# A decoder layer on one core: convolution states turned by full 128-row tiles, a padded sample residual, and engine orders fixed by tables

## The chip, the cores and the metric

The kernel runs on one core of a Trainium2 chip. The metric is device time in microseconds (us) of one launch. Three runs of the kernel before took 900.96, 899.11 and 896.12 us, so 899.11 us in the median. The profiled execution is a fourth one.

TensorE is called PE here, VectorE DVE, ScalarE ACT, GpSimd POOL and SyncE SP; PEld is PE's loading of the operand that stays in the array.

## What is computed

One layer of a hybrid decoder for a prompt of 512 tokens and 8 sample tokens (one new token for each of 8 sequences), width 1024, all in fp32. Cut to its frame:

```python
# x: prompt (1, 512, 1024) and sample (8, 1, 1024); the two groups share all weights
u = x @ w_in                                 # queries, keys, values, gates of both mixers
nsa = sparse_attention(u)                    # compressed, selected and window branches, ALiBi
qkv, gdn_conv = causal_dwconv(u_qkv, state_gdn_conv, width=4)     # state: 3 rows of 1536 per sequence
gdn, gdn_state = gated_delta_net(silu(qkv), state_gdn)            # 8 heads of 64, chunks of 64
x = layer_norm(ALPHA * x + concat(nsa, gdn) @ w_out)
h, ffn_conv = causal_dwconv(x @ w_up, state_ffn_conv, width=3)    # state: 2 rows of 2816 per sequence
x = layer_norm(ALPHA * x + (gelu(h) * gate) @ w_down)
x = layer_norm(ALPHA * x + per_layer_embedding(x, p))
# outputs: x, key/value rows, windows, delta-net states, the new rows of both convolutions
```

## The kernel before

**Layout.** Activations lie with features on the partitions and the 520 tokens along the columns, in two halves: half 0 has 256 columns (prompt), half 1 has 264 (256 of the prompt and the 8 samples). The weights come from HBM by feature tiles of 128.

**Products.** An fp32 product is made of three products in the faster type float32r. `wtile` casts a weight tile to `wh` (ACT, L210 or L199) and subtracts to get the rest `wl` (DVE or POOL, L211 or L200). `product` then does for each 128 rows of the contraction wh·xh (L355), wl·xh (L356) and wh·xl (L359). The steps that carry a page row name `mm` are these. Small products are left in fp32, which the trace shows as two records each.

**Order.** The work is written as a list of steps in two strings: `ORDER` (input projection tiles G and D, attention steps, delta-net steps K, g, C, X, s, v, then w_out) and `TAIL` (w_down tiles D, norms M, the embedding P and B, the last norm and the outputs). A table `do` calls a function for each step. That written order is not the order on the engines: `kernel` opens the tile framework with its scheduler, which reorders the written instructions of each engine by its own estimates and inserts the waits. Each engine then runs its own fixed list.

**Places that the change touches.**
- L266-267: the first piece of the delta-net's convolution state, 24 rows of 512, is loaded. `conv_state` (L401-409) loads the other two, turns each by four transposes of 24 rows x 128 columns (L408) into one PSUM tile `gstT`, and copies that to `gst`. `gdn_tile` calls it at its tiles 0, 4 and 8.
- `residual` (L1271-1281) adds ALPHA·x to an output tile inside PSUM, between two of the w_out steps: two fp32 products with 128 token rows against ALPHA times the identity `aid` (L1278, four records), and in half 1 one with the 8 sample rows (L1280, two records). There are 8 output tiles in each half. `delta_half` (L1283-1292) loads the sample rows as two tiles `xs` of 8 rows.
- `ffn_state` (L1346-1356) loads the ConvFFN's state as six pieces of 16 rows, turns it by 22 transposes of 16 rows x 128 columns (L1354) and copies each piece from PSUM (DVE, L1355, six copies).
- Three further places are only moved: the delta-net's key products `kk` on 32 rows (L589, L591), the norms (`mu` L1229, subtraction L1233, squares `lsq` L1235, `var` L1241, `rstd` L164, scaling L1250, the casts `x1h` L1252 and `x1l` L1254), and the delta-net's chunk steps on 64 rows (`vn` L763, `S` L769, `o` L784 and L792, `val` L719, `kcd` L728, `qk` L743, and the transposes of the keys and values L874).

Of the kernel before, what the change touches and what calls it, by code (L numbers as in the profile page):

```python
# [23 lines left out]
HA = 256  # L24
HEADS = 8
FF = 2816
NFT = FF // 128
# [70 lines left out]
SUB, EVAC = 'VVVVVVVV VVVVVVVV VVVVVVVV VVVVVVVV VVVVVVVV'.split(), 'VVVVVVVV VVVVVVVV'.split()  # L98
TAIL = 'D00 D10 D11 D12 D01 D13 D14 D15 D16 D17 M1 D02 P0 D03 D04 D05 B0 D06 B1 D07 B2 P1 M0 B3 B4 L B5 R0 B6 B7 T00 T01 Z E3 U0 R1 T10 T11 T12 U1 E2 E4'


def body(tc, nc, ctx, I, O, dbg=None):
# [22 lines left out]
    def PS(name, tag):  # L125
        nid[0] += 1
        return pp.tile([128, 512], F32, tag=tag, name=f"{name}_{nid[0]}", bufs=BANKS[tag])
# [19 lines left out]
    def r3(ap, n):  # L147
        return ap.rearrange("p (a b) -> p a b", a=n)
# [116 lines left out]
    rows_v = feature_rows()  # L265
    st_first = UV("st24", [24, 512])  # L266
    nc.sync.dma_start(st_first, I["state_gdn_conv"][0].rearrange("b r c -> (b r) c")[:, 512:1024])
    w_first = [([], [])]
# [128 lines left out]

    gst = UV("gst", [128, 12, 24])
    gstv = gst.rearrange("p j (b r) -> p j b r", r=3)

    def conv_state(hf):  # L401
        st = st_first
        if hf != 1:
            st = UV("st24", [24, 512])
            nc.sync.dma_start(st, I["state_gdn_conv"][0].rearrange("b r c -> (b r) c")[:, hf * 512:(hf + 1) * 512])
        ps = PS("gstT", "pn")
        for j in range(4):
            PE.transpose(ps[:, j * 24:(j + 1) * 24], st[:, j * 128:(j + 1) * 128], ident[:24, :24])  # L408
        V.tensor_copy(gst[:, hf * 4:(hf + 1) * 4, :], r3(ps[:, :96], 4))

# [50 lines left out]
    def gdn_tile(j, ws=None):  # L461
# [4 lines left out]
        if not F:  # L466
            vectors()
        if j % 4 == 0:
            conv_state(j // 4)
        gcw = F["gcw"]  # L470
# [803 lines left out]
    def residual(o, hv, rows):  # L1274

        def add(_, ps):
            for s2 in range(2):
                PE.matmul(ps[:, s2 * 128:s2 * 128 + 128], rows[:, s2 * 128:s2 * 128 + 128], L["aid"], start=False, stop=False)  # L1278
            if hv == 1:
                PE.matmul(ps[:, HA:HA + 8], xsrow[o], L["aid"][:8, :8], start=False, stop=False)  # L1280
        return add

    def delta_half(hv, tag):  # L1283
        if "aid" not in L:
            L["aid"] = UV("aid", [128, 128])
            G.tensor_scalar(L["aid"], ident, ALPHA, None, op0=ALU.mult)
        if hv == 1:
            rs_ = [UV("xs", [8, 512], "g") for c in range(2)]
            for c in range(2):
                nc.sync.dma_start(rs_[c], I["x_sample"][:, 0, c * 512:(c + 1) * 512])  # L1290
            xsrow[:] = [rs_[k // 4][:, k % 4 * 128:k % 4 * 128 + 128] for k in range(8)]
        split_mix(hv, tag, 1)
        R[hv] = by_halves("R", hv, "g")
# [52 lines left out]
    def ffn_state():  # L1346
        fst = UV("fst", [128, NFT, 16])
        for c0 in range(0, NFT, 4):
            n = min(4, NFT - c0)
            st = UV("st16", [16, 512])  # L1350
            nc.sync.dma_start(st[:, :n * 128], I["state_ffn_conv"][0].rearrange("b r c -> (b r) c")[:, c0 * 128:(c0 + n) * 128])
            ps = PS("fstT", "pg")
            for j in range(n):
                PE.transpose(ps[:, j * 16:(j + 1) * 16], st[:, j * 128:(j + 1) * 128], ident[:16, :16])  # L1354
            V.tensor_copy(fst[:, c0:c0 + n, :], r3(ps[:, :n * 16], n))  # L1355
        FS["v"] = fst.rearrange("p j (b r) -> p j b r", r=2)

# [290 lines left out]
```

## Time and profile before

| what | value |
|---|---|
| three runs | 900.96, 899.11, 896.12 us (median 899.11) |
| the profiled execution's own time | 898.38 us |
| its span (first to last instruction) | 896.4 us |
| its mean granted TensorE clock | 0.982 of full speed |
| PE busy | 862.4 us, 96% of the span |
| PEld busy | 804.2 us, 90% |
| DVE busy | 576.5 us, 64% |
| ACT busy | 426.8 us, 48% |
| POOL busy | 194.3 us, 22% |
| busy share of the 16 DMA engines, first queue | 32.6% |

How to read it: the time of a run is the span and about 2 us around it. Busy times are unions of instruction spans; a PE instruction's span is longer than the distance to the next one, since products are pipelined, so prices on PE are read as distances between starts. PEclk is the clock that was granted; 1.00 is full speed and 0.50 half.

### The profile page before, as it was taken

To read this page: it belongs to the slowest core of one execution; us is meant where nothing else is said; L and a number is where in the kernel's file an instruction comes from. 1 tells how busy PE (TensorE), PEld (TensorE's weight loads), DVE (VectorE), ACT (ScalarE), POOL (GpSimd) and SP (SyncE) were. 2 spreads that over 40 slices of the span, in tenths; PEclk is the share of its full clock that TensorE was granted. 3 is DMA by queue.
4 is the path that set the end of the run, shared out by engine and by line. 5 is a ranking of instruction groups with operands and counts; after the bars stand their busy time and mean duration, and the time that the engine had idled before them with its cause. 6 is when DMAs were issued, how large, how long until landed. Compare 5 with 4: busy or idle time off the path is not lost.

```text
span 896.4 us, 19333 instructions
## 1 busy us (share of the span) xinstructions
PE 862.4 (96%) x7689; PEld 804.2 (90%) x7689; DVE 576.5 (64%) x1317; ACT 426.8 (48%) x940; POOL 194.3 (22%) x301
## 2 busy tenths in 40 slices
PE   8999999999998989999999999999999999998995
PEld 6989998988897757979999999999999999998984
DVE  3788994576769787778655553345543345577967
ACT  4555546333447885645644432244431244434744
POOL 1241231362404432206720000000000000005333
PEclk9999999899999999989999999999999999999998
DMA  7322323332237230333413333333343134352202
GB/s 222 86 54 72 92 78 81 91 85 61 67 85 242 73 100 13 108 113 92 142 60 119 106 97 94 97 113 102 93 119 95 55 89 119 92 157 82 95 1 96
DMA packets 138550, 85.93 MB, mean 96 GB/s; under 512 B 8354, under 2 KB 129940, under 8 KB 138316
## 3 DMA queue, kind: packets, MB, share of 16 engines
q1 hardware_dynamic: 138460, 84.70, 32.6%
q8 instruction: 60, 0.98, 0.5%
q14 instruction: 30, 0.25, 0.1%
HBM read 79.48 MB, written 7.36 MB: 97 GB/s over the span
## 4 chain that ended last, share of the span: by engine, by line
PE 75%; DVE 9%; DMA 7%; ACT 5%; issue 2%; POOL 2%; SPq 1%; DVEq 0%; POOLq 0%; ACTq 0%
PE mm L355 19%; PE mm L359 18%; PE mm L356 18%; DMA wn<-in_state_nsa_win_dram 2%; PE PT L992 2%; DVE wl L211 1%; DMA praw<-in_ple_w_gate_dram 1%; DMA raw<-in_ffn_w_down_dram 1%; PE var L1241 1%; DMA raw<-in_w_out_dram 1%; PE O L999 1%; DVE R L1250 1%; PE O L1000 1%; DMA raw<-in_ffn_w_up_dram 1%; PE S L956 1%
## 5 line engine op out<-in xcount | busy, mean ns | idle before, releaser
L211 DVE TENSOR_TENSOR wl<-raw,wh 128x512 fp32r<-128x512 f32 (+1 forms) x190 | 132.5, 700 | 131.0 <-ACT wh L210 129.9
L210 ACT CAST wh<-raw 128x512 fp32r<-128x512 f32 x198 | 120.3, 612 | 189.6 <-PE mm L359 152.3
L356 PE MATMUL mm<-x1h,wl 128*128 128x256 f32 (+1 forms) x704 | 199.0, 283 | 0.4 <-POOL wl L211 0.4
L359 PE MATMUL mm<-x1l,wh 128*128 128x256 f32 (+1 forms) x704 | 198.7, 283 | 0.0
L355 PE MATMUL mm<-x1h,wh 128*128 128x256 f32 (+1 forms) x704 | 198.4, 283 | 0.0
L356 PEld LDWEIGHTS mm<-x1h,wl 128*128 128x128 f32 x704 | 132.1, 188 | 0.9 <-POOL wl L211 0.8
L359 PEld LDWEIGHTS mm<-x1l,wh 128*128 128x128 f32 x704 | 132.6, 188 | 0.1
L355 PEld LDWEIGHTS mm<-x1h,wh 128*128 128x128 f32 x704 | 132.5, 189 | 0.1
L355 PE MATMUL mm<-xh,wh 128*128 128x264 f32 (+1 forms) x408 | 120.4, 295 | 1.7 <-ACT xh L329 1.0
L359 PE MATMUL mm<-xl,wh 128*128 128x264 f32 (+1 forms) x408 | 118.8, 291 | 0.0
L356 PE MATMUL mm<-xh,wl 128*128 128x264 f32 (+1 forms) x408 | 118.3, 290 | 0.0
L356 PE MATMUL mm<-hhl,wl 128*128 128x256 f32 (+1 forms) x352 | 100.0, 286 | 0.0
L355 PE MATMUL mm<-hhl,wh 128*128 128x264 f32 (+1 forms) x352 | 100.0, 286 | 0.0
L359 PE MATMUL mm<-hhl,wh 128*128 128x256 f32 (+1 forms) x352 | 99.7, 286 | 0.0
L355 PEld LDWEIGHTS mm<-xh,wh 128*128 128x128 f32 x408 | 78.9, 193 | 3.7 <-ACT xh L329 1.1
L359 PEld LDWEIGHTS mm<-xl,wh 128*128 128x128 f32 x408 | 78.8, 193 | 0.9 <-issue 0.5
L356 PEld LDWEIGHTS mm<-xh,wl 128*128 128x128 f32 x408 | 78.8, 193 | 0.8 <-issue 0.5
L1392 POOL COPY last<-fcb 128x10 f32<-128x10 f32 x22 | 4.9, 225 | 307.9 <-ACT fcb L1380 296.5
L355 PEld LDWEIGHTS mm<-hhl,wh 128*128 128x128 f32 x352 | 66.9, 191 | 0.2
L356 PEld LDWEIGHTS mm<-hhl,wl 128*128 128x128 f32 x352 | 66.9, 190 | 0.2
L359 PEld LDWEIGHTS mm<-hhl,wh 128*128 128x128 f32 x352 | 66.5, 190 | 0.2
L1255 POOL TENSOR_SCALAR R<-R,vec 128x264 f32<-128x264 f32 (+1 forms) x40 | 32.2, 817 | 49.9 <-ACT x1h L1252 34.6
(450 smaller groups left out, 1879.4 us busy)
## 6 DMA issues: line engine op xcount, KB each, us to landing
raw<-in_ffn_w_up_dram SPq DMA_DIRECT2D x44, 512.0 KB
raw<-in_w_in_dram SPq DMA_DIRECT2D x25, 512.0 KB
raw<-in_w_out_dram SPq DMA_DIRECT2D x32, 256.0 KB
raw<-in_ffn_w_down_dram SPq DMA_DIRECT2D x16, 512.0 KB
pg<-in_cache_nsa_kv_dram SPq DMA_DIRECT2D x16, 256.0 KB
praw<-in_ple_w_gate_dram SPq DMA_DIRECT2D x8, 512.0 KB
raw<-in_ffn_w_down_dram SPq DMA_DIRECT2D x8, 384.0 KB
xr<-in_x_prompt_dram SPq DMA_DIRECT2D x16, 128.0 KB
```

What stands on the lines that cost most here:

```text
L210: both = (S.copy(th[:, :k1 - k0, :M], raw[:, k0:k1, :M]), low.tensor_tensor(tl[:, :k1 - k0, :M], raw[:, k0:k1, :M], th[:, :k1 - k0, :M], o ...
L211: low.tensor_tensor(tl[:, :k1 - k0, :M], raw[:, k0:k1, :M], th[:, :k1 - k0, :M], op=ALU.subtract))
L355: PE.matmul(o, hs[k], rh[hv][k], start=(k == ks[0]), stop=False)
L356: PE.matmul(o, ls[k], rh[hv][k], start=False, stop=False)
L359: PE.matmul(o, hs[k], rl[hv][k], start=False, stop=(k == ks[-1]))
L956: PE.matmul(ps[:, :wm], q_[:, ts_], kh[:, :wm], start=True, stop=False)
L992: PE.transpose(pt[:, g4 * 128:g4 * 128 + 128], P[g4][:, st * 128:st * 128 + 128], ident)
L999: PE.matmul(po, VV[br][:, st, kv, :], pT_[0][:, :512], start=(br == 0 and st == 0), stop=False)
L1000: PE.matmul(po, VV[br][:, st, kv, :], pT_[1][:, :512], start=False, stop=(br == 1 and st == tt))
L1241: PE.matmul(pv[:, :n], C("onesm"), sq_[:, :n], start=(k < grp), stop=(k == 7))
L1250: V.scalar_tensor_tensor(r, r, lng[:, i, k:k + 1], rstd[:, :n], op0=ALU.mult, op1=ALU.mult)
L1255: G.tensor_scalar(r, r, b_, 1.0, op0=ALU.add, op1=ALU.mult)
```

## The change

It has four parts.

1. The delta-net's convolution state is seen as 288 rows of 128 and turned by three transposes of 128 full rows (they overlap: rows 0, 128 and 160 on), at once, at the head of the program; the loads are three transfers of 128 x 128. Two copies take the result out of PSUM. The view `gstv` changes to fit.
2. The ConvFFN's state likewise: 352 rows of 128, three loads, three transposes, two copies.
3. The sample residual's tiles `xs` get 128 rows: POOL zeroes them, the load fills the first 8, and the product takes all 128 rows.
4. `in_order` takes for each of the five engines a string of steps through the written instructions (`RUNS`) and chains that engine's instructions in this order with dependencies that need no semaphore. A second loop chains the first uses of the buffers of each tag in written order.

```diff
+RUNS = dict(
+    PE='+0*60 +24 +1*2 -3 +2 -29*7 +22 -23*6 +17*2 -19*9 +10*2 -12 +11*3 -14 +13*53 ...
+    ...
+)
+
+def in_order(tc, nc):
+    of = dict(PE=mybir.EngineType.PE, ...)
+    written = [i for i in nc.cur_bb.bb.instructions if ...]
+    for e, text in RUNS.items():
+        mine = [i for i in written if i.engine == of[e]]
+        at, last = 0, None
+        for run in text.split():
+            step, _, n = run.partition("*")
+            at += int(step)
+            for _ in range(int(n or 1)):
+                if last is not None:
+                    tc.add_manual_dep(mine[at], last, ..., reason="order")
+                last = mine[at].name
+                at += 1
+    seen, of_tag = set(), {}
+    for i in written:
+        for a in list(i.ins) + list(i.outs):
+            ...
+            if tag in of_tag and of_tag[tag] is not i:
+                tc.add_manual_dep(i, of_tag[tag].name, ..., reason="slot")
+            of_tag[tag] = i
...
-    st_first = UV("st24", [24, 512])
-    nc.sync.dma_start(st_first, I["state_gdn_conv"][0].rearrange("b r c -> (b r) c")[:, 512:1024])
+    def state_rows(src, n, name):
+        st = UV(name, [128, 3, 128])
+        at = (0, 128, n - 128)
+        for i, a_ in enumerate(at):
+            nc.sync.dma_start(st[:, i], src[a_:a_ + 128, :])
+        return st, at
+
+    def state_turned(out, rows, name, tag):
+        st, at = rows
+        ps = PS(name, tag)
+        for i, a_ in enumerate(at):
+            PE.transpose(ps[:, i * 128:i * 128 + 128], st[:, i], ident)
+        m = at[2]
+        V.tensor_copy(out[:, :256], ps[:, :256])
+        V.tensor_copy(out[:, 256:m + 128], ps[:, 512 - m:384])
+
+    gst_rows = state_rows(I["state_gdn_conv"][0].rearrange("b r (j p) -> (b r j) p", p=128), 288, "gst_rows")
...
-    def conv_state(hf):
-        ...
-        for j in range(4):
-            PE.transpose(ps[:, j * 24:(j + 1) * 24], st[:, j * 128:(j + 1) * 128], ident[:24, :24])
-        V.tensor_copy(gst[:, hf * 4:(hf + 1) * 4, :], r3(ps[:, :96], 4))
...
         if not F:
             vectors()
-        if j % 4 == 0:
-            conv_state(j // 4)
+            state_turned(gst, gst_rows, "gstT", "pn")
...
-                PE.matmul(ps[:, HA:HA + 8], xsrow[o], L["aid"][:8, :8], start=False, stop=False)
+                PE.matmul(ps[:, HA:HA + 8], xsrow[o], L["aid"][:, :8], start=False, stop=False)
...
-            rs_ = [UV("xs", [8, 512], "g") for c in range(2)]
+            rs_ = [UV("xs", [128, 512], "g") for c in range(2)]
             for c in range(2):
-                nc.sync.dma_start(rs_[c], I["x_sample"][:, 0, c * 512:(c + 1) * 512])
+                G.memset(rs_[c], 0.0)
+                nc.sync.dma_start(rs_[c][:8], I["x_sample"][:, 0, c * 512:(c + 1) * 512])
...
     def ffn_state():
-        fst = UV("fst", [128, NFT, 16])
-        for c0 in range(0, NFT, 4):
-            ...
-        FS["v"] = fst.rearrange("p j (b r) -> p j b r", r=2)
+        fst = UV("fst", [128, NFT * 16])
+        state_turned(fst, state_rows(I["state_ffn_conv"][0].rearrange("b r (j p) -> (b r j) p", p=128), NFT * 16, "fst_rows"), "fstT", "pg")
+        FS["v"] = fst.rearrange("p (b r j) -> p j b r", b=8, r=2)
...
         body(tc, nc, ctx, I, O)
+        in_order(tc, nc)
```

In the tables of order below, L589 and L591 of before are L634 and L636 of the change, L355, L356 and L359 are L411, L412 and L415, the transposes L408 and L1354 are L318, and in the norms L1219, L1233, L1250, L1254, L1468, L1500 are L1264, L1278, L1295, L1299, L1507, L1539. The number behind a tile's name tells one tile from another and differs between the two kernels. Counted over the whole order, PE has 6785 products before and 6757 in the change; products of another array shape than the one ahead of them (128 rows and columns, or 64, or 32 and so on) are 199 before and 144 in the change. In the delta-net's stage the longest run of PE products without an `mm` step between has 77 of them before and 126 in the change.

**PE, the first delta-net chunks' key products.** `kk` are the key products of two chunks, on 32 of the array's rows; `mm` are the input projection's steps. Before:

```order
L355 MATMUL mm_1190<-xh_7_78,wh_1182 128x256
L589 MATMUL kk_682<-qkv_368 32x32
L591 MATMUL kk_682<-qkv_368 32x64
L356 MATMUL mm_1190<-xh_7_78,wl_1183 128x256
...
L578 MATMUL exps_676<-rr_672,cst 128x256
L550 MATMUL gc_611<-gm_614,cst 128x64
L589 MATMUL kk_682<-qkv_442 32x32
L579 MATMUL exps_676<-rr_672,cst 128x256
L591 MATMUL kk_682<-qkv_442 32x64
L408 MATMUL gstT_1161<-cst,st_128_1159 128x24 x4
L356 MATMUL mm_1190<-xh_11_82,wl_1187 128x256
```

and now:

```order
L412 MATMUL mm_1284<-xh_15_86,wl_1255 128x264
L415 MATMUL mm_1284<-xh_15_86,wh_1254 128x264
L634 MATMUL kk_683<-qkv_295 32x32
L636 MATMUL kk_683<-qkv_295 32x64
L634 MATMUL kk_684<-qkv_295 32x32
L636 MATMUL kk_684<-qkv_295 32x64
L634 MATMUL kk_683<-qkv_370 32x32
```

Before, the first two chunks' products come in five pieces among the large ones; now all 32 of them stand in one row, and the four transposes of `gst` are gone from among them.

**PE, the end of attention.** `PT` and `O` are the transposed probabilities and their products with the values, `fstT` is the ConvFFN's state, `mm_5718` is an output tile of w_out. Before:

```order
L992 MATMUL PT_5654<-cst,P_5446 128x128
L1354 MATMUL fstT_5776<-cst,st_949_5774 128x16 x4
L1354 MATMUL fstT_5784<-cst,st_951_5782 128x16 x4
L999 MATMUL O_5598<-PTh_5648,VV_2678 128x512
L1000 MATMUL O_5598<-PTl_5649,VV_2678 128x512
L999 MATMUL O_5598<-PTh_5659,VV_2678 128x512
```

and now:

```order
L411 MATMUL mm_5718<-mh_810_5167,wh_5714 128x256
L318 MATMUL fstT_5758<-cst,fst_rows_5754 128x128 x3
L412 MATMUL mm_5718<-mh_810_5167,wl_5715 128x256
L415 MATMUL mm_5718<-ml_812_5169,wh_5714 128x256
L411 MATMUL mm_5718<-mh_810_5167,wh_5714 128x256
L1045 MATMUL O_5586<-PTl_5593,VV_2377 128x512
L1044 MATMUL O_5586<-PTh_5603,VV_2377 128x512
```

Before, the last `PT` and `O` steps stand with only the state's small transposes between them; now the state is three rows, and steps of w_out stand between the attention's.

**DVE, the norm of half 1 after w_down.** `R` are the rows of the residual sum, `acc` their sum over tiles, `mu` the mean, `wl` parts of the embedding's weights. Before:

```order
L1219 TENSOR_TENSOR acc_10319<-acc_10319,R_524_3928 128x264
L1500 TENSOR_TENSOR wl_10636<-praw_2_10632,wh_10634 128x2x512
L1468 TENSOR_TENSOR R_399_3211<-R_399_3211,mm_10654 128x256
L1233 TENSOR_TENSOR R_521_3925<-R_521_3925,mu_10529 128x264 x2
...
L1250 SCALAR_TENSOR_TENSOR R_521_3925<-R_521_3925,vec,rstd_10564 128x264 x2
L1250 SCALAR_TENSOR_TENSOR R_522_3926<-R_522_3926,vec,rstd_10564 128x264 x2
L1250 SCALAR_TENSOR_TENSOR R_523_3927<-R_523_3927,vec,rstd_10564 128x264 x2
L1250 SCALAR_TENSOR_TENSOR R_524_3928<-R_524_3928,vec,rstd_10564 128x264 x2
L1254 SCALAR_TENSOR_TENSOR x1l_1015_6092<-R_521_3925,vec,x1h_1011_6088 128x264
```

and now:

```order
L1264 TENSOR_TENSOR acc_10271<-acc_10271,R_520_3916 128x264
L1539 TENSOR_TENSOR wl_10576<-praw_0_10572,wh_10574 128x2x512
L1278 TENSOR_TENSOR R_517_3913<-R_517_3913,mu_10481 128x264 x2
...
L1295 SCALAR_TENSOR_TENSOR R_518_3914<-R_518_3914,vec,rstd_10516 128x264 x2
L1295 SCALAR_TENSOR_TENSOR R_517_3913<-R_517_3913,vec,rstd_10516 128x264
L1299 SCALAR_TENSOR_TENSOR x1l_1002_6045<-R_518_3914,vec,x1h_998_6041 128x264
L1295 SCALAR_TENSOR_TENSOR R_519_3915<-R_519_3915,vec,rstd_10516 128x264
```

The first `x1l` came behind all eight scalings and now comes behind three; between `acc` and the subtraction of the mean stood a part of the weights and an update of the other half, and now only a part of the weights. On PE, 48 steps stand between the norm's last `var` and the first step that takes an `x1l`; they are mostly steps of w_down for the other half.

## Rows read from the trace of the kernel before

**Rows 1.** The page: the span, the busy time of each engine with its share and instructions, the granted clock by 40 slices in tenths, and the chain that ended last by engine.

```profile
span 896.4 us, 19333 instructions
...
PE 862.4 (96%) x7689; PEld 804.2 (90%) x7689; DVE 576.5 (64%) x1317; ACT 426.8 (48%) x940; POOL 194.3 (22%) x301
...
PEclk9999999899999999989999999999999999999998
...
PE 75%; DVE 9%; DMA 7%; ACT 5%; issue 2%; POOL 2%; SPq 1%; DVEq 0%; POOLq 0%; ACTq 0%
```

**Rows 2.** The table by stretches. Columns: the stretch in us, its length, then busy us (x instructions) of PE, PEld, DVE, ACT and POOL, the granted clock, the DMA share, GB/s.

```profile
440.00:800.00 360.00, 360.00 (x3008) 359.82 (x3007) 177.90 (x345) 135.37 (x243) 16.16 (x55) 1.00 0.34 100
157.10:163.90 6.80, 6.80 (x79) 6.14 (x75) 4.10 (x6) 2.53 (x5) 3.35 (x3) 0.50 0.65 175
171.00:177.60 6.60, 6.60 (x165) 6.11 (x163) 5.17 (x10) 2.71 (x6) 0.94 (x3) 1.00 0.25 62
204.90:208.30 3.40, 3.40 (x19) 3.40 (x17) 1.97 (x3) 0.00 (x0) 0.00 (x0) 0.50 0.58 170
396.00:402.90 6.90, 6.90 (x27) 4.98 (x26) 4.43 (x11) 2.82 (x7) 0.00 (x0) 0.51 0.27 80
819.30:822.70 3.40, 3.40 (x18) 3.40 (x17) 3.40 (x5) 1.77 (x2) 3.40 (x5) 0.50 0.00 0
```

**Rows 3.** What PE waited for. Columns: engine, operation and line <- releaser: us in total, times, longest.

```profile
PE S L956 <- DVE mn L963: 2.6, 6, 0.8
PE mm L1543 <- DVE x1l L1254: 2.4, 1, 2.4
PE kvT L874 <- ACT kvf L868: 1.9, 1, 1.9
PE val L719 <- DVE vb L714: 1.7, 1, 1.7
...
PE fstT L1354 <- DVE PTl L998: 1.4, 1, 1.4
...
PE var L1241 <- ACT lsq L1235: 1.3, 2, 0.8
PE mt L443 <- DVE mT L437: 1.3, 1, 1.3
...
PE o L792 <- DVE vn L763: 1.0, 1, 1.0
```

**Rows 4.** PE's timeline at the end of attention. Columns here and in the groups of timelines below: start us, duration us, engine, line, operation, tiles, shapes, count, and in brackets the idle time before it.

```profile
390.40 0.42 PE L1354 MATMUL fstT<-cst,st 16*128 16x16 f32 x4
...
394.87 0.64 PE L1354 MATMUL fstT<-cst,st 16*128 16x16 f32 x8 [1.37 <-DVE PTl L998]
...
397.42 1.03 PE L1354 MATMUL fstT<-cst,st 16*128 16x16 f32 x8
...
399.96 0.39 PE L1354 MATMUL fstT<-cst,st 16*128 16x16 f32 x2
```

**Rows 5.** PE's timeline: transposes of full 128 rows at the head, and the third piece of the delta-net's state among steps of 0.12 us.

```profile
13.05 1.91 PE L291 MATMUL xT<-cst,xr 128*128 128x128 f32 x16
...
77.13 0.28 PE L359 MATMUL mm<-xl,wh 128*128 128x264 f32 x1
77.34 0.42 PE L408 MATMUL gstT<-cst,st 24*128 24x24 f32 x4
77.70 0.39 PE L355 MATMUL mm<-xh,wh 128*128 128x256 f32 x1
```

**Rows 6.** PE's timeline: one residual of half 0, without a sample, and one of half 1, with it.

```profile
250.15 0.61 PE L1278 MATMUL mm<-aid,xr 128*128 128x128 f32 x4
250.51 0.36 PE L359 MATMUL mm<-ml,wh 128*128 128x256 f32 x1
...
353.38 0.60 PE L1278 MATMUL mm<-aid,xr 128*128 128x128 f32 x4
353.91 0.38 PE L1280 MATMUL mm<-aid,xs 8*128 8x8 f32 x2
354.22 0.40 PE L359 MATMUL mm<-ml,wh 128*128 128x264 f32 x1
```

**Rows 7.** PE's timeline: the second of the five pieces of `kk`.

```profile
56.77 0.28 PE L355 MATMUL mm<-xh,wh 128*128 128x256 f32 x1
56.98 0.21 PE L589 MATMUL kk<-qkv 64*32 64x32 f32 x1
...
57.21 0.39 PE L356 MATMUL mm<-xh,wl 128*128 128x256 f32 x1
57.44 0.28 PE L359 MATMUL mm<-xl,wh 128*128 128x256 f32 x1
```

**Rows 8.** DVE's timeline in the norm of half 1 after w_down.

```profile
800.93 0.43 DVE L1219 TENSOR_TENSOR acc<-acc,R 128x264 f32<-128x264 f32 x1
803.14 1.23 DVE L1500 TENSOR_TENSOR wl<-praw,wh 128x1024 fp32r<-128x1024 f32 x1 [1.78 <-ACT wh L1497]
...
804.62 2.80 DVE L1233 TENSOR_TENSOR R<-R,mu 128x264 f32<-128x264 f32 x8
...
812.41 5.29 DVE L1250 SCALAR_TENSOR_TENSOR R<-R,vec,rstd 128x264 f32<-128x264 f32 x8 [0.32 <-ACT rstd L164]
817.62 0.71 DVE L1254 SCALAR_TENSOR_TENSOR x1l<-R,vec,x1h 128x264 fp32r<-128x264 f32 x1
```

More of the change, by code (lines that the diff above doesn't have):

```diff
@@ new lines, in in_order @@
+def in_order(tc, nc):
+    of = dict(PE=mybir.EngineType.PE, ACT=mybir.EngineType.Activation, DVE=mybir.EngineType.DVE,
+              POOL=mybir.EngineType.Pool, SP=mybir.EngineType.SP)
+    written = [i for i in nc.cur_bb.bb.instructions if type(i).__name__ not in ("BassTilePoolBoundary", "InstRegisterAlu", "InstSeqAssert")]
+    for e, text in RUNS.items():
[6 more added lines that the diff above has]
+                if last is not None:
+                    tc.add_manual_dep(mine[at], last, mybir.DependencyInfo(mybir.DependencyClass.NoSync, mybir.DependencyReason.DATA), reason="order")
+                last = mine[at].name
[3 more added lines that the diff above has]
+        for a in list(i.ins) + list(i.outs):
+            t = getattr(getattr(a, "bass_ap", None), "tensor", None)
+            tag = getattr(t, "tag", None)
+            if tag is None or t.name in seen:
+                continue
+            seen.add(t.name)
+            if tag in of_tag and of_tag[tag] is not i:
+                tc.add_manual_dep(i, of_tag[tag].name, mybir.DependencyInfo(mybir.DependencyClass.NoSync, mybir.DependencyReason.DATA), reason="slot")
+            of_tag[tag] = i
@@ L396, in body @@
     lrow = {}
-    gst = UV("gst", [128, 12, 24])
-    gstv = gst.rearrange("p j (b r) -> p j b r", r=3)
-    def conv_state(hf):
[L402 to L406, printed above, removed]
-        for j in range(4):
-            PE.transpose(ps[:, j * 24:(j + 1) * 24], st[:, j * 128:(j + 1) * 128], ident[:24, :24])
-        V.tensor_copy(gst[:, hf * 4:(hf + 1) * 4, :], r3(ps[:, :96], 4))
+    gst = UV("gst", [128, 288])
+    gstv = gst.rearrange("p (b r j) -> p j b r", b=8, r=3)
     alog, dtb = K("alog", [128, 8]), K("dtb", [128, 8])
@@ L1346, in ffn_state @@
     def ffn_state():
-        fst = UV("fst", [128, NFT, 16])
-        for c0 in range(0, NFT, 4):
[L1349 to L1355, printed above, removed]
-        FS["v"] = fst.rearrange("p j (b r) -> p j b r", r=2)
+        fst = UV("fst", [128, NFT * 16])
+        state_turned(fst, state_rows(I["state_ffn_conv"][0].rearrange("b r (j p) -> (b r j) p", p=128), NFT * 16, "fst_rows"), "fstT", "pg")
+        FS["v"] = fst.rearrange("p (b r j) -> p j b r", b=8, r=2)
     unit = lambda a: tuple(int(c) for c in a)
```

5 lines of the change are left out of this document (added).

## The prediction

> **What bounds the kernel now.** I read the page first. PE is busy for 862.4 of 896.4 us, and the chain that ended last runs through PE for 75% of the span [rows 1]; the reader is to see that only 34.0 us of the span are not PE work, and that the next engine, DVE, has 576.5 us. So the time falls only if PE does fewer or cheaper steps, waits less, or gets a better clock. Then I read the table by stretches [rows 2]. From 440 to 800 us PE is busy for 360.00 of 360.00 us at a clock of 1.00: 40% of the kernel, the ConvFFN, in which no order gains anything. What can be gained lies before 440 and after 800. There the clock falls to 0.50 in stretches such as 157.1 to 163.9, 204.9 to 208.3, 396.0 to 402.9 and 819.3 to 822.7 us, together 20.5 us, each of which costs about half its length. Third, the list of PE's waits [rows 3]: the eight shown add up to 13.6 us, none longer than 2.4. Last, the timelines at the places that the change edits [rows 4 to 8].
>
> The span of 896.4 us has a time of 898.38, and the median of the three runs is 899.11. I sum against 898.4 and add 0.7 at the end.
>
> **The ConvFFN's state.** Its 22 small transposes take 0.42 + 0.64 + 1.03 + 0.39 = 2.48 us of PE [rows 4], the 1.03 partly because it falls into a stretch at half clock [rows 2]. Three full ones replace them. Sixteen full transposes took 1.91 us [rows 5], so three cost 0.36. Gain 2.1 us, all on PE's path, since PE was the busy engine there. The six transfers become three; PE's waits name no state transfer [rows 3], so I cost them at nothing: the cover is the whole attention stage, and if they came late the three transposes would stand in PE's queue with w_out steps behind them. Four fewer copies free DVE at a place where PE waited 1.37 us for DVE's `PTl` [rows 4].
>
> **The delta-net's state.** Among steps 0.12 us apart, four small transposes put 77.70 - 77.13 = 0.57 us between two steps [rows 5], so 0.45 us for a piece. Two pieces lie in the middle of the program: 0.9 us. The first piece, at the head, becomes three full transposes, 0.36 us by the row above, which replaces about as much. Gain 0.9.
>
> **The sample residual.** A residual without the sample takes 250.51 - 250.15 = 0.36 us to the next step, one with it 354.22 - 353.38 = 0.84 [rows 6]. So the two records of the sample cost 0.48 us. With full rows they keep the array's shape. The four records of the prompt take 0.36 us and have 128 columns, so two with 8 columns cost at most half of that, 0.18, and I take 0.22 with something for a load of the array; the bounds are 0.1 and 0.48. Gain 8 x 0.26 = 2.1 us (0 to 3.0). The trace thus says that the price lies in the change of shape, not in the rows. The Trainium skill has a rule that speaks against this edit: by "TensorE: Matmul & The Clock Gate", section "Why this matters for your kernels", a single product of 32 rows takes as long as one of 128, and few rows pay only where several products run side by side in the array, so padding alone earns nothing. By that rule the sum would be 16.4 - 2.1 = 14.3 us. The prompt products beside the sample's [rows 6], which are short and full, decide for me.
>
> POOL's two added zeroings stand ahead of two loads at the start of half 1. POOL is busy for 194.3 us of 896.4 [rows 1], so I cost them at nothing; if a load came late, the sample product would wait inside an open output tile, with all of PE's w_out steps behind it.
>
> **Grouping.** The second piece of `kk` shows the price of a change of shape: the step into it is 56.98 - 56.77 = 0.21 us instead of 0.12, and the step after it 57.44 - 57.21 = 0.23 instead of 0.12 [rows 7]. So a change costs about 0.1 us. The order has 199 of them before and 144 now. Of these 55, 34 belong to the removed pieces (6 to the delta-net's state, 12 to the ConvFFN's, 16 to the residual) and are paid above. The other 21 give 21 x 0.1 = 2.1 us (bounds 1 and 3). The upper bound would be a change on both sides of a group that another shape follows, the lower one changes that fall into a wait and cost nothing.
>
> **The norm of half 1 after w_down.** `acc` ends at 801.36, yet the subtraction starts only at 804.62, behind a `wl` at 803.14 and an update; the first `x1l` starts at 817.62, behind eight scalings of 5.29 us in all [rows 8]. PE waits 2.4 us for it [rows 3], then runs at 0.50 for 3.4 us [rows 2], which costs 1.7. In the new order the subtraction follows `acc` after one `wl` of 1.2 us, some 2 us earlier, and the first `x1l` stands behind three scalings, not eight: 5 x 0.66 = 3.3 us earlier. That is 5.3 us against a wait of 2.4, and 48 steps of 0.12 us (5.7 us) stand as cover between the last `var` and it. So I take the whole wait and its slow stretch: 2.4 + 1.7 = 4.1 us.
>
> **Other waits.** `mt` (1.3 us) [rows 3] now stands after a whole tile of 24 steps (2.9 us): covered, 1.3. The wait ahead of `fstT` (1.4 us) [rows 3] was a chain of `PT`, its two parts on ACT and DVE, and `O`, with nothing of PE's between; w_out steps now stand there: 1.4. The stretch at half clock behind it, worth about 3.4 us, I leave for the range. The delta-net's and compression's waits `S`, `kvT`, `val` and `o` add up to 7.2 us [rows 3]. `val` and `kvT` have more before them now, but `vn` and `S` form a chain from chunk to chunk that no order shortens. I take a third, 2.4 us; the bounds are 7.2 and a loss of as much, if a table fixed from other durations than the chip's puts a late operand ahead of ready steps.
>
> **Sum.** 2.1 + 0.9 + 2.1 + 2.1 + 4.1 + 1.3 + 1.4 + 2.4 = 16.4 us. 898.4 - 16.4 = 882.0, and by the median 882.7.
>
> **Rivals.** *Only the removed work counts.* The products saved are certain, the waits move: a fixed order that is earlier at one place is late at the next. Then 2.1 + 0.9 + 2.1 + 2.1 = 7.2 remain: 891.9. For it speaks that waits of 13.6 us were left by an order made with the same freedom; against it that the norm's gain has 5.3 us of slack for 2.4.
>
> *The waits go altogether and the clock stays up.* 7.2, the 13.6 of the list and half of the 20.5 us of half clock, 10.2, give 31 us: 868. For it speaks that every slow stretch named follows or holds waits or few products; against it the chain of `vn` and `S`, and that a stretch such as 157.1 to 163.9 holds 79 instructions in unbroken work and is slow all the same.
>
> *Slower: longer runs of small products lower the clock.* The place is the delta-net's stage, before 440 us: its products on 64 rows and its transposes now stand in runs of up to 126 without a step of a large product between, 77 before. If such runs put PE to half clock, each stretch like 157.1 to 163.9 [rows 2] costs 3.4 us more. Four of them beside the waits that stay make 891.9 + 13.6 = 905.5; the case decides from four on. Against it stands one row: 171.0 to 177.6 is 6.6 us with 165 PE instructions, so nearly all small ones, at a clock of 1.00. For it: 157.1 to 163.9 at 0.50. The Trainium skill's "TensorE: Matmul & The Clock Gate", Part 4, says that transposes do not count as PE work for the clock in the same way; the trace here has both answers for runs of small products, and no run shows which holds for a longer one.
>
> *The change does not group.* If the tables only rewrote the scheduler's order, 5.1 us of removed pieces would remain: 894.0. The order on PE, with 144 changes of shape for 199, speaks against it.
>
> **How the numbers follow.** A measurement of this kernel can tell about 0.5% from no change, that is 4.5 us: faster is below 894.6, slower above 903.6. My forecast, 882.7 with a range of its own from 873 to 890, has 0.55; all waits gone 0.13; only the removed work 0.17, of which most lies below 894.6; no grouping 0.05; slower 0.10. Faster is then 0.55 + 0.13 + 0.09 = 0.77, same the other 0.08 and 0.05, 0.13, slower 0.10. The range of 8 in 10 goes from 866, the second rival with a little more, to 899, where no waits are won and part of the removed work is eaten.
>
> **What would show it.** Right: PE busy falls by some 7 us; no wait of `x1l` in the norm; `fstT` a single row of 0.4 us; sample residuals 0.22 us apart; fewer stretches at 0.50. Wrong: new lines in PE's waits of more than 2 us, above all for a transfer or for `vb`, `vn` or a `wl` that the table put too late; a mean clock below 0.98; or an end of attention that is as thin as before.

## The result

The change takes 884.89 us in the median of four runs (884.35 to 887.08), the kernel before 898.63. The ratio is 0.9852 (interval 0.9821 to 0.9884). Six more runs of the change, among the experiments, gave 885.74 in the median and a ratio of 0.9864 (0.9830 to 0.9898); over all ten runs the median is 885.0. So of the 16.4 us forecast some 13 were gained: 13.7 against the runs of the kernel before that stand beside the first four, 10.7 against those beside the six more (median 896.44). The forecast time of 882.7 us is missed by 2 to 3 us, inside the range of 866 to 899.

The page of the change, the span, the busy times and the granted clock, against [rows 1]:

```profile
span 885.1 us, 19223 instructions
...
PE 850.9 (96%) x7661; PEld 793.1 (90%) x7661; DVE 585.3 (66%) x1312; ACT 426.8 (48%) x940; POOL 198.4 (22%) x303
...
PEclk9999999999999999999999999999999999999999
```

PE's busy time fell by 11.5 us, the span by 11.3. So outside its products PE stands still as long as before; how much of the 11.5 is less work and how much a better clock is taken apart below. The stretches of the change, against [rows 2], with the columns of that group:

```profile
430.00:790.00 360.00, 359.22 (x2984) 357.94 (x2983) 178.89 (x339) 135.74 (x245) 21.57 (x54) 1.00 0.33 98
19.30:22.70 3.40, 3.40 (x18) 3.40 (x18) 1.77 (x5) 1.18 (x3) 0.00 (x0) 0.50 0.88 254
265.00:268.40 3.40, 3.38 (x16) 3.38 (x17) 3.29 (x14) 2.63 (x10) 1.49 (x2) 0.50 0.30 81
205.20:208.20 3.00, 0.32 (x4) 0.12 (x2) 2.94 (x5) 0.89 (x2) 2.92 (x3) 1.00 0.56 164
208.20:212.00 3.80, 3.80 (x33) 3.73 (x34) 3.13 (x5) 1.23 (x4) 0.77 (x4) 1.00 0.00 0
```

The ConvFFN's stretch is full but for 0.8 us. Ahead of PE's last products, the change has two stretches at half clock, 6.8 us; the kernel before had five, 23.9 us (the four of [rows 2] and one behind the first weights). The last two rows belong together: PE waits for nearly all of the stretch at 205.2, and the clock stays at 1.00 behind it. What PE waited for, against [rows 3]:

```profile
PE so L874 <- DVE inn L790: 2.7, 1, 2.7
PE S L1001 <- DVE mn L1008: 2.2, 3, 1.1
PE mm L411 <- ACT R L1349: 2.2, 2, 1.9
...
PE kk L634 <- DVE Lb L643: 1.5, 2, 1.3
PE gstT L318 <- DMA gst_rows<-in_state_gdn_conv_dram: 1.5, 1, 1.5
PE mu L1274 <- DVE acc L1264: 1.4, 1, 1.4
PE gc L591 <- DVE g L588: 1.1, 1, 1.1
PE var L1286 <- ACT lsq L1280: 1.1, 2, 0.6
```

The reader is to see that of the lines of [rows 3] only `S` and `var` are left (and 0.2 us of `val`), and that others took their place: `so`, the copy of `R` on ACT, `kk`, `gstT`, `gc`. Summed over all its lines the list gives 26.5 us before and 26.9 in the change. With `so` and the copy of `R` one of the prediction's signs of being wrong is there, new lines of more than 2 us, beside its signs of being right. PE's timeline at the two places where pieces were removed, against [rows 4] and [rows 6]:

```profile
384.90 0.36 PE L411 MATMUL mm<-mh,wh 128*128 128x256 f32 x1
385.11 0.49 PE L318 MATMUL fstT<-cst,fst_rows 128*128 128x128 f32 x3
385.35 0.36 PE L412 MATMUL mm<-mh,wl 128*128 128x256 f32 x1
...
347.72 0.61 PE L1323 MATMUL mm<-aid,xr 128*128 128x128 f32 x4
348.17 0.27 PE L1244 MATMUL oST<-cst,osb 128*128 128x128 f32 x1
348.28 0.29 PE L1325 MATMUL mm<-aid,xs 128*128 128x8 f32 x2
348.42 0.37 PE L415 MATMUL mm<-ml,wh 128*128 128x264 f32 x1
```

The ConvFFN's state now takes one row, 0.24 us to the next step. The sample's two records take 348.42 - 348.17 = 0.25 us with a small product beside them, for 0.48 in [rows 6]. The head, against [rows 5]:

```profile
17.07 0.26 PE L440 MATMUL vec<-cst,vr 49*128 49x49 f32 x1
18.82 0.33 PE L318 MATMUL gstT<-cst,gst_rows 128*128 128x128 f32 x1 [1.49 <-DMA gst_rows<-in_state_gdn_conv_dram]
18.91 0.37 PE L411 MATMUL mm<-xh,wh 128*128 128x264 f32 x1
```

Here the third transpose waits 1.49 us for its transfer, and the first product of the second tile starts at 18.91 us, where it started at 17.29 before. The wait is not all of that: the transpose `xsT` of the sample rows, ahead of it, starts at 16.02 us for 14.90 before. And DVE in the norm of half 1 after w_down, against [rows 8]:

```profile
793.83 0.44 DVE L1264 TENSOR_TENSOR acc<-acc,R 128x264 f32<-128x264 f32 x1
794.18 1.22 DVE L1539 TENSOR_TENSOR wl<-praw,wh 128x1024 fp32r<-128x1024 f32 x1
795.32 2.80 DVE L1278 TENSOR_TENSOR R<-R,mu 128x264 f32<-128x264 f32 x8
...
802.78 1.30 DVE L1295 SCALAR_TENSOR_TENSOR R<-R,vec,rstd 128x264 f32<-128x264 f32 x3 [1.20 <-ACT rstd L203]
804.00 0.49 DVE L1299 SCALAR_TENSOR_TENSOR x1l<-R,vec,x1h 128x264 fp32r<-128x264 f32 x1
```

From the end of `acc` (794.26) the subtraction starts 1.1 us later, for 3.3 before, and the first `x1l` ends 10.2 us later, for 17.0. PE does not wait for it.

### The profile page after: what moved, and what is told of

It reads as the page before. It is cut to its first block, busy times and chain, and to the rows that moved or that the text cites. A ratio compares the mean times of both kernels' runs of the same rounds, so it can differ in the third digit from the quotient of the medians.

```text
span 885.1 us, 19223 instructions
## 1 busy us (share of the span) xinstructions
PE 850.9 (96%) x7661; PEld 793.1 (90%) x7661; DVE 585.3 (66%) x1312; ACT 426.8 (48%) x940; POOL 198.4 (22%) x303
## 4 chain that ended last, share of the span: by engine, by line
PE 70%; DVE 16%; ACT 5%; DMA 4%; issue 3%; POOL 1%; SPq 1%; DVEq 0%; ACTq 0%
PE mm L411 18%; PE mm L415 18%; PE mm L412 18%; DVE wl L250 2%; DMA raw<-in_w_out_dram 2%; DVE R L1295 1%; PE PT L1037 1%; DVE qkv L519 1%; DVE X L655 1%; PE S L1001 1%; PE var L1286 1%; DMA raw<-in_w_in_dram 1%; PE pgate L1615 1%; PE pgate L1617 1%; DVE KHL L974 1%
## 5 line engine op out<-in xcount | busy, mean ns | idle before, releaser
L411 PE MATMUL mm<-x1h,wh 128*128 128x256 f32 (+1 forms) x704 | 195.7, 285 | 0.6 <-ACT fcb L1419 0.6
L412 PE MATMUL mm<-x1h,wl 128*128 128x264 f32 (+1 forms) x704 | 195.7, 283 | 0.2 <-POOL wl L250 0.2
L415 PE MATMUL mm<-x1l,wh 128*128 128x264 f32 (+1 forms) x704 | 195.6, 283 | 0.0
L411 PEld LDWEIGHTS mm<-x1h,wh 128*128 128x128 f32 x704 | 131.1, 188 | 1.6 <-ACT fcb L1419 0.8
L412 PEld LDWEIGHTS mm<-x1h,wl 128*128 128x128 f32 x704 | 131.7, 188 | 0.5 <-POOL wl L250 0.4
L415 PEld LDWEIGHTS mm<-x1l,wh 128*128 128x128 f32 x704 | 131.5, 188 | 0.0
L411 PE MATMUL mm<-xh,wh 128*128 128x256 f32 (+1 forms) x408 | 118.7, 298 | 0.3 <-DVE mT L483 0.2
L412 PE MATMUL mm<-xh,wl 128*128 128x264 f32 (+1 forms) x408 | 115.2, 286 | 0.0
L415 PE MATMUL mm<-xl,wh 128*128 128x264 f32 (+1 forms) x408 | 114.3, 286 | 0.0
L412 PE MATMUL mm<-hhl,wl 128*128 128x256 f32 (+1 forms) x352 | 97.9, 283 | 0.0
L411 PE MATMUL mm<-hhl,wh 128*128 128x264 f32 (+1 forms) x352 | 97.0, 284 | 0.3 <-DVE R L1507 0.3
L415 PE MATMUL mm<-hhl,wh 128*128 128x256 f32 (+1 forms) x352 | 96.7, 283 | 0.0
L411 PEld LDWEIGHTS mm<-xh,wh 128*128 128x128 f32 x408 | 76.8, 190 | 4.5 <-ACT z L203 0.7
L1431 POOL COPY last<-fcb 128x10 f32<-128x10 f32 x22 | 8.9, 405 | 310.5 <-ACT fcb L1419 294.7
L412 PEld LDWEIGHTS mm<-xh,wl 128*128 128x128 f32 x408 | 77.1, 190 | 0.8 <-issue 0.5
L415 PEld LDWEIGHTS mm<-xl,wh 128*128 128x128 f32 x408 | 76.9, 190 | 0.4 <-issue 0.2
L412 PEld LDWEIGHTS mm<-hhl,wl 128*128 128x128 f32 x352 | 65.7, 188 | 0.1
L411 PEld LDWEIGHTS mm<-hhl,wh 128*128 128x128 f32 x352 | 65.3, 188 | 0.5 <-DVE R L1507 0.5
L415 PEld LDWEIGHTS mm<-hhl,wh 128*128 128x128 f32 x352 | 65.2, 188 | 0.1
L1300 POOL TENSOR_SCALAR R<-R,vec 128x264 f32<-128x264 f32 (+1 forms) x40 | 28.7, 730 | 67.9 <-ACT x1h L1297 50.3
```

Source lines behind the costliest of these rows:

```text
L411: PE.matmul(o, hs[k], rh[hv][k], start=(k == ks[0]), stop=False)
L412: PE.matmul(o, ls[k], rh[hv][k], start=False, stop=False)
L415: PE.matmul(o, hs[k], rl[hv][k], start=False, stop=(k == ks[-1]))
L1300: G.tensor_scalar(r, r, b_, 1.0, op0=ALU.add, op1=ALU.mult)
L1431: G.tensor_copy(rows[:, :, f % 4], cb[:, 512:522])
```

## The experiments

**The edits without the tables.**

```diff
         body(tc, nc, ctx, I, O)
-        in_order(tc, nc)
```

> The change without its order tables: full-row turns of both states and the padded sample residual, and the scheduler orders the engines as it did before. The theory: most of the 13.7 us gained came with the tables, through the clock (half-clock stretches before the end fell from 23.8 to 6.8 us, worth 8.5 us), while the removed pieces are worth about 5 us at most. Then this kernel takes 890 to 897 us and keeps most of the half-clock stretches. The rival: the removed small transposes were what lowered the clock and made the chain at the end of attention thin, and the tables add little. Then it takes 884 to 888 us with under 10 us at half clock. A third possibility is that the scheduler's new order is worse at another place, over 899 us.

890.9 us (888.8 to 895.7, ten runs), ratio 0.9922 (0.9890 to 0.9955). Its page and three of its waits:

```profile
span 888.8 us, 19257 instructions
...
PE 849.8 (96%) x7661; PEld 795.0 (89%) x7661; DVE 575.7 (65%) x1312; ACT 426.8 (48%) x940; POOL 192.3 (22%) x303
...
PE cmpo L1075 <- DVE mix L1076: 3.4, 1, 3.4
PE O L1007 <- ACT PTh L1005: 3.3, 4, 1.7
...
PE mm L1545 <- DVE x1l L1262: 2.4, 1, 2.4
```

So the three edits gain 7.7 us and the tables some 5.9 more. The scheduler made a new order for the edited program, and the 7.7 hold what that gained or lost. The `x1l` wait of 2.4 us is back (its line is L1545 here), and the end of attention waits in `O` and `cmpo`. Half clock before the last products: 10.2 us. PE is busy for 1.1 us less than in the change. The time is the theory's, 890 to 897; "most of the half-clock stretches" is not, since 10.2 of 23.9 us are left. As in the change, PE does not wait for `fstT`.

**The residual on 8 rows again.**

```diff
-                PE.matmul(ps[:, HA:HA + 8], xsrow[o], L["aid"][:, :8], start=False, stop=False)
+                PE.matmul(ps[:, HA:HA + 8], xsrow[o][:8], L["aid"][:8, :8], start=False, stop=False)
```

> The change with the sample residual's product on 8 rows again, all else and all orders the same (the zeroing stays). The theory of the prediction's third term: each of the 8 residuals loses 0.2 to 0.26 us again, so 2 us in all: ratio to the change about 1.0023, and in the trace 0.48 us instead of about 0.25 around the product. The rival, that few rows cost the same as many: no difference, within 0.3 us.

887.41 us (885.4 to 889.4, four runs); with intervals of some 0.6% that does not tell 2 us from none. In its trace the two records lie between 347.50 and 348.01, 0.51 us for the 0.25 of the change. The next two kernels measure the same price eight times as large.

**64 products of few and of full rows where PE never waits.** Each adds zero inside a product tile of the ConvFFN; `zz` is a tile of zeros, 128 x 8.

```diff
             if extra and k == ks[0]:
                 extra(hv, ps)
+            if "ffn" in F and k == ks[0] and len(dums) < 64:
+                dums.append(0)
+                PE.matmul(o[:, :8], ident[:8, :M], zz[:8], start=False, stop=False)    # or ident[:, :M], zz
```

> The change plus 64 products of 8 rows by 8 columns that add zero, one inside each of 64 product tiles of the ConvFFN, behind its second step, where TensorE never waits. It measures the price of an 8-row product alone. From the residual's rows, 0.48 us each, so 31 us more than the change. The rival, that few rows cost as much as many: the same as with 128 rows.

> The same 64 added products with 128 rows by 8 columns. The prediction took 0.22 us each, so 14 us more than the change; the rule that a product of few rows takes as long as one of 128 expects the same as the kernel with 8 rows.

916.44 us with 8 rows (915.6 to 919.2) and 899.66 with 128 (896.6 to 902.2): against 885.74 of the change beside them, 30.7 / 64 = 0.48 us and 13.9 / 64 = 0.22 us for each. The groups of the added products, 8 rows and then 128 (count, busy us and mean ns as on the page):

```profile
L420 PE MATMUL mm<-zz,cst 8*128 8x8 f32 x128 | 24.6, 262 | 0.0
```

```profile
L420 PE MATMUL mm<-zz,cst 128*128 128x8 f32 x128 | 18.1, 214 | 0.0
```

Their own durations differ by 48 ns a record only. In the traces near 561 us the step into the added product is 0.21 us with 8 rows and 0.12 with 128, the product itself 0.31 and 0.14 to the next step, and that next step 0.23 and 0.21. So the price of an 8-row product between full ones is shown. That it is the change of the array's shape, and not the few rows, is argued from [rows 4], where eight 16-row transposes behind each other take 0.64 us; no run has 8-row products behind each other. The rule weighed in the prediction, the Trainium skill's "TensorE: Matmul & The Clock Gate", section "Why this matters for your kernels", is for a product by itself, which no run here times; between full products padding gains 0.26 us, and the measurement decides. The Trainium skill's "TensorEngine Tiling (Array Packing)", Key Properties, says that changing the tiling mode drains TensorE; the longer steps of 0.21 and 0.31 us agree with it, though no row names the mode.

**The norm with its casts behind all eight scalings, and also with a later subtraction.** DVE's order, the second kernel with both pieces:

```diff
 acc, wl
+R, wl
 R - mu (eight)
-R, wl, wl, scale, scale, scale, x1l, scale, x1l, scale, R, scale, x1l, scale, ...
+wl, scale (eight), x1l, R, x1l, x1l, R, R, x1l, x1l, x1l
```

> The change, with DVE's order in the norm of half 1 after w_down set back: all eight scalings first, then the casts x1l. The theory of the prediction's norm term: the first x1l ends near 808.8 us of the trace instead of 804.5, TensorE waits about 2 us for it and may then run at half clock for 3.4 us, so 2 to 4 us longer than the change, 887 to 889 us. The rival, that the steps of w_down on TensorE cover it anyway and the gain came from the earlier subtraction and the grouped var: under 0.5 us.

> The change with DVE's order in the norm of half 1 after w_down set back further: behind the sum of the rows come one more weight part and an update before the subtraction of the mean (1.6 us later), and all eight scalings before the first x1l (3.3 us later). The theory by the prediction's own terms: the new order has 5.3 us of slack for a wait of 2.4, so 2.9 to spare; 1.6 + 3.3 = 4.9 us taken away leave a wait of about 2 us at the first step with x1l (the kernel with the 3.3 alone showed 0.7). The rival, that TensorE's order covers it at any rate: under 1 us.

The first took 888.32 us (884.6 to 890.3, ten runs), against 885.0 for the change. That is inside the forecast 887 to 889, but the ratios to the kernel before, 0.9887 (0.9856 to 0.9918) and 0.9864 (0.9830 to 0.9898), overlap, and its profiled execution was shorter than the change's (span 883.8): the times do not tell. The second has one run, 884.92 us. The traces tell more: PE waits 0.7 us for `x1l` in both. DVE in the second kernel, and the wait:

```profile
793.38 2.79 DVE L1278 TENSOR_TENSOR R<-R,mu 128x264 f32<-128x264 f32 x8
...
799.98 3.47 DVE L1295 SCALAR_TENSOR_TENSOR R<-R,vec,rstd 128x264 f32<-128x264 f32 x8 [1.14 <-ACT rstd L203]
803.37 0.48 DVE L1299 SCALAR_TENSOR_TENSOR x1l<-R,vec,x1h 128x264 fp32r<-128x264 f32 x1
...
PE mm L1582 <- DVE x1l L1299: 0.7, 1, 0.7
```

With the subtraction as late as before (3.2 us behind `acc`) and all scalings first, the first `x1l` still ends 3.3 us earlier than before, 13.7 us behind `acc`. So the edit took back 3.4 of the 6.7 us that the change had gained here, not the 4.9 expected. The eight scalings took 3.47 us here for 5.29 in [rows 8], and the squares on ACT run unbroken in both kernels, where casts of `pwh` stood among them before. Of the 3.3 us, 1.8 are the scalings' and 1.2 lie between subtraction and scalings. The forecast wait of 2 us did not come: the DVE order that the prediction named did not remove the wait of 2.4 us alone.

**Five moves, each of a waiting instruction behind ready work.**

```diff
 PE:   mm (end of a tile)
-so, so, so, mm (24 steps), oT
+mm (24 steps), so, so, so, oT
 ACT:  R copy
-x1h, R copy
+R copy, x1h
 PE:   gstT, gstT, vec
-gstT, mm (24 steps)
+mm (24 steps), gstT
 ACT:
-sq, sq, cb copy, sq, cb copy
+cb copy, cb copy (ahead of the casts), sq, sq, sq
 PE:
-l2, gc, l2, mm (25 steps); kk (32), mm (7 steps)
+mm (11), l2, mm (14), gc, l2; mm (7 steps), kk (32)
```

> The change with five moves in its tables, each taking an instruction that waits away from in front of ready work. (1) TensorE's three sample products so, which waited 2.7 us, go behind the 24 ready steps after them. (2) On ACT one copy of R goes ahead of an x1h that waits for DVE (TensorE waited 1.9 us for it). (3) The third state transpose at the head goes behind 24 steps (waited 1.5 us), its DVE copies behind the weights. (4) Two evacuation copies cb on ACT go ahead of the square roots of the key norm, and TensorE's ready steps ahead of gc and the second l2 (waits of 1.1, 0.9 and about 1 us). (5) Seven product steps go ahead of the key products kk that waited 1.3 us. The theory: waits in a fixed order are instructions in front of ready work, and each wait that is taken out shortens the program by its length: 2.7 + 1.9 + 0.8 + 2 + 0.8, about 8 us, so 877 us. The rival: what follows is bound by the same engines behind and the waits turn up later, 883 to 886 us.

885.32 us (884.1 to 886.6): the same as the change, and not the 877 expected. Its longest wait, the stretch ahead of it with the columns of [rows 2], and what ACT did there:

```profile
PE mm L411 <- ACT kvf L913: 2.2, 1, 2.2
...
200.00:205.00 5.00, 2.94 (x24) 2.73 (x24) 4.92 (x6) 0.76 (x2) 4.86 (x6) 1.00 0.60 157
...
204.25 0.63 ACT L840 ACTIVATE osq<-o 128x512 f32<-128x512 f32 x1 [5.58 <-DVE o L838]
204.78 0.35 ACT L913 COPY kvf<-mm 128x256 f32<-128x256 f32 x1
```

`so` no longer waits, but the 24 steps put ahead of it do, 2.2 us, for a bank that ACT frees. DVE is busy for 4.92 and POOL for 4.86 of the 5.0 us before, and ACT for 0.76 only. The last product that the copy `kvf` reads ends at 202.94, so its input is there; but ACT's table has `osq` ahead of it, which waits for DVE's `o` until 204.25. So the wait that moved comes from ACT's order, where the copy stands behind an instruction that waits. Whether the copy can go ahead of `osq` and PE then runs on, or meets the chain of DVE and POOL next, was not tried. Of the others two stayed ahead in the trace for a while: the program was 1.2 us further after the `cb` copies and 2.0 after the `R` copy, of which 0.9 to 1.2 were lost again within 20 us.

> Two of the five moves of the earlier kernel alone, those after which its trace stayed ahead of the change: the two evacuation copies and the product steps near 52 to 56 us (1.2 us ahead afterwards), and the copy of R ahead of x1h near 408 us (2.0 us ahead, 0.9 to 1.2 of it given back some ten us later). The theory: about 2.4 us, so 882 to 883 us where the change took 885 (median of its ten runs 885.0, 884.2 to 889.1). The rival: both are given back where DVE or ACT is behind, as with the three other moves, and it is the same as the change, 884 to 886 us.

886.18 us (883.3 to 889.0): the rival held here too. No kernel of this record is faster than the change.

**Both kernels once more.**

> The change itself once more, as the base for the others and for a second profile of it. Expected 884 to 887 us; the theory that the clock carries most of what the removed pieces do not carry expects again under 8 us at half clock before the end; the rival, that the number of slow stretches is chance from run to run, expects anything from 3 to 25.

> The kernel before once more, one profile. The theory: stretches at half clock of some 20 us before the end, at the same places as in its first profile (behind the first weights, in the chunk steps near 157 and 205, at the end of attention near 396, in the norm near 819). The rival, chance from run to run: at other places, or under 10 us.

The change's second profile has 13.6 us at half clock before its last products (6.8 in the first), the kernel before 17.0 (23.9), near 18 and 158 us as in its first and at 240, but not at the end of attention nor in the norm. So "under 8 us" was missed, and the rival, chance, holds in part. At `so` the change waits 2.7 us in both executions; here is what follows in the second, with the columns of [rows 2]:

```profile
205.20:207.50 2.30, 0.10 (x1) 0.00 (x0) 2.27 (x3) 0.87 (x2) 2.22 (x3) 0.99 0.66 198
207.50:214.30 6.80, 6.29 (x31) 6.17 (x32) 3.59 (x6) 1.15 (x4) 1.29 (x4) 0.50 0.00 0
```

The same wait at the same place was followed by 3.8 us at 1.00 in the first profile and by 6.8 us at 0.50 in the second. Over the eight profiles that have this wait (2.7 to 2.8 us), a slow stretch follows in three. In the nine profiles of kernels with all five tables (0 to 13.6 us) the slow stretches lie at four places only, near 20, 207, 236 and 265 us, at each in three or four profiles. So their number is partly chance and partly the order's.

The record also has each run's mean granted clock, and there the order's share is plain: 0.985 over 58 runs of the kernel before (0.978 to 0.994), 0.994 over the ten of the change. The times go with the clock: eight runs of before at 0.990 and above took 891.3 to 895.3 us, thirteen at 0.981 and below 899.1 to 903.8.

**One side of the tables.** The table of PE alone, and those of the other four engines alone.

```diff
 RUNS = dict(
     PE=...,
-    ACT=..., DVE=..., POOL=..., SP=...,     # the other kernel: PE=... left out instead
 )
```

> The change with the order table of TensorE alone (and the buffers' order); ACT, DVE, POOL and SP are ordered by the scheduler. Known so far: the change takes about 885, without any table 891. The theory: what the tables gain, some 5 to 6 us, comes from waits of TensorE for DVE and ACT at a few places (the wait of 2.4 us and its slow stretch in the norm, the chain at the end of attention), so both sides of such a place must be moved: TensorE's table alone keeps half of it, 887 to 890 us. The rival, that the grouping on TensorE alone carries it: 884 to 886 us. Another: the scheduler's other engines do not fit that fixed order and TensorE waits more, over 893 us.

> The change with the tables of ACT, DVE, POOL and SP and without TensorE's. The theory: the norm's earlier subtraction lies in DVE's table, the cover for it in TensorE's; 886 to 890 us, and TensorE has fewer changes between kinds of products than with its table, so its busy time falls by 1 to 3 us. The rival, that TensorE's grouping carries the gain: 890 us or more.

930.04 us (927.3 to 933.6) and 939.42 us (938.2 to 943.8): both far slower than before, ratios 1.0326 and 1.0456. The third possibility named for PE's table alone, that the orders do not fit, has the direction; nothing forecast had the size. PE alone, and then the four others alone, with their longest waits:

```profile
span 931.8 us, 19254 instructions
...
PE mm L1576 <- DVE sg L1556: 7.6, 1, 7.6
PE mu L1270 <- DVE acc L1260: 6.9, 2, 4.7
```

```profile
span 936.6 us, 19194 instructions
...
PE 872.1 (93%) x7661; PEld 807.1 (86%) x7661; DVE 583.9 (62%) x1312; ACT 425.0 (45%) x940; POOL 201.0 (21%) x303
...
PE mm L410 <- ACT kvf L912: 7.2, 1, 7.2
```

PE's waits sum to 58.4 and 56.7 us, for 26.9 with all tables, and there are 47.6 and 34.0 us at half clock before the last products. Without its table, PE's busy time did not fall by 1 to 3 us but rose by 21, in part by the clock. The longest waits suggest that one engine's fixed order meets the scheduler's order of the others, and each waits for what the other has put later. Of the sets tried only the whole one works.

## Why the prediction was right, and where not

The sum came out near, in part by luck: its parts are wrong in ways that cancel. To separate them I take half of each slow stretch off PE's busy time, which leaves PE's work at full clock: 862.4 - 11.9 = 850.5 us before (850.3 in its second profile), 849.8 - 5.1 = 844.7 with the edits alone, 850.9 - 3.4 = 847.5 with the change (846.8 in its second). As means of two profiles each the span fell by 9.8 us: 5.1 by the clock, 3.3 by PE's work, 1.4 by PE's standing still less. The forecast had 1.7, 7.2 and 7.5.

- **The removed pieces**, 2.1 + 0.9 + 2.1 = 5.1 us forecast: the edits alone cut PE's work by 5.8, so the size holds. The residual's 0.22 us was measured as 0.22 by the added products. The turned state of the ConvFFN was tried only together with the others.
- **The head**, costed at nothing: the first product starts 1.6 us later. The prediction looked at PE's work there and not at the three transfers that now stand in SP's queue behind others; the wait for `gstT` of 1.5 us is theirs. It is not the whole loss: 1.1 us are there at `xsT` already, and with the third transpose moved away (the five moves) the first product starts at 18.51 us, waiting for ACT's `xh`.
- **Grouping**, 2.1 us forecast: against the edits alone, the tables add 2.1 to 2.8 us of PE work. It is not that they interrupt the large products more often. The first `mm` step behind other work is late alike: 106 of them lose 11.3 us with the edits alone and 108 lose 11.5 in the change, outside slow stretches. The loss lies within rows of `mm`: 3 steps longer than 0.14 us with the edits alone, 0.3 us over their 0.12, and 48 and 46 in the change's two profiles, 4.3 and 4.2 us. Here is one, with the columns of [rows 4]:

```profile
444.11 0.28 PE L415 MATMUL mm<-x1l,wh 128*128 128x264 f32 x1
444.29 0.39 PE L411 MATMUL mm<-x1h,wh 128*128 128x256 f32 x1
444.51 0.27 PE L412 MATMUL mm<-x1h,wl 128*128 128x256 f32 x1
```

  The steps are 0.18 and 0.22 us for 0.12, where one half's output tile ends and the next begins. Such stops are too short for the list of waits, and the term had no place for them; what PE waits for there is not shown. Without them PE's work falls by 1.2 to 1.8 us from the edits alone to the change, so the term itself may hold; nothing tests it alone. Its count was off: in the traces the edits alone take out 21 changes of shape, not 34, and the tables the other 34.
- **The norm**, 4.1 us forecast: the wait of 2.4 is gone, so that size holds. The 1.7 for a slow stretch behind it was one execution's: the second profile of before has the same wait and none behind it. The working does not hold either: with DVE's order of before, 0.7 of the wait came back, and the first `x1l` was still 3.3 us earlier than before. The table of ACT, which leaves the squares unbroken, and POOL's play a part that was not taken apart.
- **The other waits**, 5.1 us forecast: with the norm's, 7.5 us of waits were to go. The list's sum went from 26.5 and 29.0 us in the two profiles of before to 26.9 and 25.9, so 1.4 as a mean. `mt`, `fstT`, `kvT` and nearly all of `val` and `o` went, but most came back elsewhere, which is the first rival's mechanism. The wait ahead of `fstT` was read as a chain of `PT` and `O`, which w_out steps would cover. The second profile of before shows another cause:

```profile
396.29 0.69 DVE L998 TENSOR_TENSOR PTl<-PT,PTh 128x512 fp32r<-128x512 f32 x1
...
396.86 0.64 PE L1354 MATMUL fstT<-cst,st 16*128 16x16 f32 x8 [1.46 <-DMA st<-in_state_ffn_conv_dram]
```

  `fstT` starts before `PTl` ends, when the state's transfer has landed. In both profiles five of the six loads are issued only from 3.4 to 3.5 us ahead of it; in the change all three are issued from 8.4 us ahead. So the state's earlier transfers, costed at nothing, most likely took this wait away; with the edits alone it is gone too.
- **The clock**, of which only 1.7 us were taken: half-clock time fell from 17.0 and 23.9 to 6.8 and 13.6 us, which is (20.4 - 10.2) / 2 = 5.1 us, as a mean of two profiles each. The mean clocks of all runs agree. Twice what is missing to 1, times the span, is the time at half clock: 26.4 us for the runs of before and 10.6 for the change's. By the profiles 9.7 and 3.0 of it lie at the very end, so my estimate is (16.7 - 7.6) / 2 = 4.6 us. This made up for the waits. The range had it, the sum did not. What decides whether a wait lowers the clock stays open, since one place did both.

The rival that long runs of small products lower the clock fell. The longest run in the delta-net's stage, 126 products without an `mm` among them, lies between 170.6 and 180.7 us in the change. The stretch around it, with the columns of [rows 2]:

```profile
150.00:190.00 40.00, 39.67 (x652) 36.01 (x646) 25.98 (x47) 16.20 (x34) 13.18 (x13) 1.00 0.29 73
```

PE is busy throughout and the clock stays at 1.00. None of the nine profiles with all tables has a stretch at half clock between 24 and 200 us, where both profiles of before have one near 158.

## What to carry to other kernels

Price a small product by the step after it: between full products an 8-row one costs 0.48 us and one padded to 128 rows 0.22. A wait in a fixed order names the first instruction that meets a late operand; moving it away mostly moved the wait here, so look first whether the other engine is busy, or holds a ready instruction behind one that waits. Shorter stops than the list of waits shows are found as steps longer than their neighbours'. Do not fix the order of one engine against a scheduler's order of the others: half of a set that gained 5.9 us cost 45 to 54 us against the whole.

## What the hardware showed that was not expected

The same eight scalings on DVE, 128 x 264 in fp32, took 5.29 us in [rows 8] and 3.47 in the kernel with the late norm, 0.66 and 0.43 us each. In the first POOL worked for 2.51 us from 812.24 and in three more instructions from 815.69 on, in the second for 0.83 us only; that POOL's work is the cause was not tested. And the clock fell behind the same wait of 2.7 us in three of eight profiles and not in the other five.
